# One block of step sizes cut into three steps and moved, and the q and k evictions raised in priority

## The chip, the cores and the metric

One core of a Trainium2 chip runs the whole kernel. The metric is the device time of one execution in microseconds (us). The core has five engines that each run their own instructions in an order fixed when the program is built: PE (TensorE, matrix products and transposes), ACT (ScalarE), DVE (VectorE), POOL (GpSimd) and SP (SyncE, which issues DMAs). Matrix products land in PSUM, eight banks in all; everything else lives in SBUF or in HBM.

## The reference, cut to what matters

One layer of a hybrid encoder is applied to two sequences, a prompt of 256 tokens and a sample of 512 tokens, with a model width of 1024. Three mixers (GLA, differential attention, SSD) read the same normalised input and their outputs go through one output product; an MLP with squared relu follows.

```
h = rmsnorm(x, norm1)
gq, gk, gv, gg, glr, dq, dk, dvv, sz, sxbc, sdt = split(h @ w_in)
o_gla  = gla_mixer(gq, gk, gv, gg, glr, ...)       # gated recurrence, both directions
o_diff = diff_mixer(dq, dk, dvv, ...)              # two softmaxes, w = p0 - lam * p1
o_ssd  = ssd_mixer(sz, sxbc, sdt, ...)             # state-space recurrence, both directions
x = x + concat(o_gla, o_diff, o_ssd) @ w_out
x = x + square(relu(rmsnorm(x, norm2) @ w_mlp1)) @ w_mlp2

# in ssd_mixer: the step sizes, and the running sums of their decay inside a chunk
dt = softplus(sdt + dt_bias)                       # 8 heads forward, 8 backward
la = dt * (-exp(a_log))
acum = cumsum(la)                                  # per chunk; exp(acum), exp(acum_last - acum) are used

# in gla_mixer: the gates
logg = log_sigmoid(r @ wg + bg) / 16               # forward and backward
```

## The kernel before, in words

The 768 tokens are six tiles of 128 (NT = 6): tiles 0 and 1 are the prompt, 2 to 5 the sample. Each fp32 product is made of three passes on values split in a high and a low part (`mm3`, L98 to L100). Weights come in halves (`wr`, L146) and are split by ACT (`wh`, L134) and DVE (`wl`, L135) in `load_unit`. The in-projection makes blocks of 256 columns, either transposed (`fm_unit`, features on partitions, two halves of 384 tokens) or by token (`tm_unit`, three blocks of two tiles). Their sums lie in the three PSUM banks called `acc`; all other PSUM results share five banks called `mx`.

The order of the stages in the program is: normalise and transpose x; `gla_v(0)`; `glr_unit`, which makes `rst` (the gates' low-rank input) and `zdt` (the raw step sizes, 16 rows at partitions 96 to 111); small vectors; `ssd_dt` (the block that the change is about); `gla_gates` for the two pairs of GLA heads; `gla_qk(0)`, the recurrence `gla_core` of pair 0, then q, k, v of pair 1, the output gate `gla_gate_out` of pair 0 (with a tanh), the recurrence of pair 1; for each of two pairs of attention heads the in-projection `diff_in(p)` and the two prompt heads; then the SSD (convolution, states, chunks), the output product, the sample heads, the MLP.

This program order is a priority, not the order on an engine. A planner puts every instruction on its engine's list as soon as, by its own costs, its operands and its tiles are there, and among those that could go it takes the one that stands first in the program; `tc.high_priority()` puts what is inside it ahead. `tc.issue_after` adds an order. Once built, each engine runs its list in order and waits on semaphores.

Tiles come from rings: `t3` (4 buffers of 776 columns), `s3` (6), `in` (12, made by the function `i3`, alive for the whole kernel), `s2` (3, opened when the GLA's rings are closed). A request waits until a buffer of its ring is free.

`ssd_dt` (L503 to L564) computes from `zdt`: Abs, Exp, Ln on ACT (L507 to L509); a correction of the logarithm on DVE with one more Exp (L510 to L514); the step sizes into `stk` (L517); times A into `dtl` (L520); a scan within each tile for the running sums `dpre` (L522), the exclusive sums `dexc` (L523); copies into `stk` (L524, L525) and differences (L527, `stb` L529). It then stores the sums to HBM: `scr` (L533, L534; read later by each SSD chunk as `ar` and `er`, L671 and L672) and the chunk totals `scp` (L535), reads `scp` back broadcast to all partitions as `ptb` (L538), takes its exponent on ACT (`decs`, L543), transposes `stk` and `stb` on PE into tokens by rows (L550, L555; three `mx` banks), copies them out on ACT (`tms` L552, `tmb` L556) and makes the factors `ew` (L558 to L563). `decs`, `tms` and `ew` are used by the SSD.

`gla_gates` (L268 on): matmuls `gate` (L274) into `mx` banks, Abs and Relu (L276, L277), Exp and Ln (L278, L279) on ACT, additions and a prefix scan on DVE (L282, L257). `gla_qk` evicts q and k from PSUM on ACT (L313). `gla_core`: transposes `kTp` (L371), then seven levels in each of which DVE makes `d` (L428) and `eq` (L433), POOL makes `ek` (L438), and PE many small matmuls `att` (L412). `diff_in` evicts each block to a tile `dqk` (L761) and squares it to `dsq` (L763), both from the ring `in`; DVE normalises and rotates (L765 to L775), and SP stores it; the `dv` blocks (L782) use the same ring. `diff_head` transposes q and k (`qT`, L811), makes scores `sc` (L835, L836), their row maximum (L837), exponent (`pr`, L838), the difference (L841), its transpose `wT` (L844), the product `O`, and in the end `ss` (L859) and `rb` (L867), all in `mx` banks.

Of the kernel before, what the change touches and what calls it, by code (L numbers as in the profile page):

```python
# [13 lines left out]
AF = mybir.ActivationFunctionType  # L14
ALU = mybir.AluOpType
# [4 lines left out]
P = 128  # L20
# [22 lines left out]
def hybrid_kernel(ctx, tc, io):  # L43
    nc = tc.nc
    mm, act, dve, pool = nc.tensor.matmul, nc.scalar, nc.vector, nc.gpsimd
# [14 lines left out]
    def tag(stack, name, bufs, width, side="left"):  # L60

        pl = stack.enter_context(tc.tile_pool(name=name, bufs=bufs, side=side, reuse_waits="tile"))

        def new(nme, dtype=F32, n=T if width == 776 else width):
            return pl.tile([P, width], dtype, tag=name, name=nm(nme))[:, :n]
        return new

    i3 = tag(ctx, "in", N_IN, 776)
# [4 lines left out]
    t3 = tag(first, "t3", N_T3, 776)  # L73
    c4 = tag(first, "c4", 6, 1024)
    s3 = tag(first, "s3", N_S3, 776)
# [17 lines left out]
    def bc(ap, shape):  # L93
        return ap.to_broadcast(shape)
# [99 lines left out]
    log_ins = []  # L194
# [29 lines left out]
        return [(raw[:, :, 0:32], w_in[:, :, C_GLR:C_GLR + 32]), (raw[:, :, 32:48], w_in[:, :, C_SDT:C_SDT + 16])]  # L224

    rst = s3("rst", F32R)
    zdt = s3("zdt")

    def glr_consume(ps, ts):
        act.copy(rst[0:96, ts], ps[0:96, :])  # L230
# [14 lines left out]
        fm_unit((gh, gl), 0, 112, glr_consume, halves_)  # L245


    resetm = s3("resetm")
    pool.memset(resetm, 1.0)
    pool.memset(resetm.rearrange("p (c w) -> p c w", w=P)[:, :, 0:1], 0.0)  # L250

    def v128(t):
        return t.rearrange("p (c w) -> p c w", w=P)

    def prefix(dst, lg):

        dve.tensor_tensor_scan(dst, resetm[:dst.shape[0]], lg, 0.0, ALU.mult, ALU.add)  # L257
# [49 lines left out]
    def gla_qk(hp):  # L307
        c0 = hp * P
        q, k = i3("gq"), i3("gk")

        def keep(dst, scale):
            def consume(ps, ts):
                act.activation(dst[:, ts], ps, AF.Copy, scale=scale)  # L313
            return consume

        w = load_unit(lambda r: [(0, P, w_in[:, r, C_GQ + c0:C_GQ + c0 + P]),
                                 (P, 2 * P, w_in[:, r, C_GK + c0:C_GK + c0 + P])], (KT, 256))
        fm_unit(w, 0, P, keep(q, 0.125), halves_)
        fm_unit(w, P, P, keep(k, 1.0), halves_)
        return q, k  # L320
# [181 lines left out]

    def ssd_dt():  # L503

        ps_ = slice(96, 112)
        z, t1, u, l = zdt[ps_], t3("dz")[ps_], t3("dt2")[ps_], t3("dl")[ps_]
        act.activation(t1, z, AF.Abs)  # L507
        act.activation(t1, t1, AF.Exp, scale=-1.0)
        act.activation(l, t1, AF.Ln, bias=1.0)  # L509
        dve.tensor_scalar(u, t1, 1.0, -1.0, op0=ALU.add, op1=ALU.add)  # L510
        dve.tensor_tensor(t1, t1, u, ALU.subtract)
        act.activation(u, l, AF.Exp, scale=-1.0)
        dve.tensor_tensor(t1, t1, u, ALU.mult)
        dve.tensor_tensor(l, l, t1, ALU.add)  # L514
        stk = t3("stk")
        pool.memset(stk, 0.0)
        dve.scalar_tensor_tensor(stk[0:16], z, 0.0, l, op0=ALU.max, op1=ALU.add)  # L517
        dtl = t3("dtl")[ps_]

        dve.tensor_scalar(dtl, stk[0:16], sdtc[0:16, 3:4], -128.0, op0=ALU.mult, op1=ALU.max)  # L520
        inc, exc = t3("dpre")[ps_], t3("dexc")[ps_]
        dve.tensor_tensor_scan(inc, resetm[ps_], dtl, 0.0, ALU.mult, ALU.add)  # L522
        dve.tensor_tensor(exc, inc, dtl, ALU.subtract)  # L523
        act.copy(stk[32:48], inc)  # L524
        act.copy(stk[64:80], exc)  # L525
        tot = bc(v128(inc)[:, :, 127:128], [16, NT, P])
        dve.tensor_tensor(v128(stk[96:112]), tot, v128(inc), ALU.subtract)  # L527
        stb = t3("stb")
        dve.tensor_tensor(v128(stb[0:16]), tot, v128(exc), ALU.subtract)  # L529

        scr = dram.tile([16, T], F32, name="scr")
        scp = dram.tile([16, NT], F32, name="scp")
        nc.sync.dma_start(out=scr[0:8, :], in_=inc[0:8])  # L533
        nc.sync.dma_start(out=scr[8:16, :], in_=exc[8:16])  # L534
        nc.sync.dma_start(out=scp, in_=v128(inc)[:, :, 127])  # L535

        ptb = const.tile([P, 2, 8, NT], F32, name="ptb")
        nc.sync.dma_start(out=ptb.rearrange("p d h c -> p (d h c)"),  # L538
                            in_=bc(scp.rearrange("h c -> (h c)")[None, :], [P, 16 * NT]))
        decs = const.tile([P, NT, 2, 4], F32, name="decs")  # L540
        for g in range(2):
            gs = slice(64 * g, 64 * g + 64)
            act.activation(decs[gs], ptb[gs, :, 4 * g:4 * g + 4, :].rearrange("p d h c -> p c d h"), AF.Exp)  # L543

        tms = const.tile([P, NT, 40], F32, name="tms")
        tmb = const.tile([P, NT, 16], F32, name="tmb")
        for (a, b) in ((0, 4), (4, 6)):
            ps = mx("tms")
            for c in range(a, b):
                nc.tensor.transpose(ps[:, (c - a) * P:(c - a) * P + 112], stk[0:112, c * P:(c + 1) * P], ident[0:112, 0:112])  # L550
            for o, r, n in ((0, 0, 16), (16, 32, 8), (24, 72, 8), (32, 96, 8)):
                act.copy(tms[:, a:b, o:o + n], v128(ps)[:, :b - a, r:r + n])  # L552
        ps = mx("tmb")
        for c in range(NT):
            nc.tensor.transpose(ps[:, 16 * c:16 * c + 16], stb[0:16, c * P:(c + 1) * P], ident[0:16, 0:16])  # L555
        act.copy(tmb, ps[:, :96].rearrange("p (c r) -> p c r", c=NT))  # L556
        ew = const.tile([P, NT, 2, 2, 8], F32, name="ew")
        act.activation(ew[:, :, 0, 0, :], tms[:, :, 16:24], AF.Exp)  # L558
        act.activation(ew[:, :, 0, 1, :], tmb[:, :, 8:16], AF.Exp)
        act.activation(ew[:, :, 1, 0, :], tms[:, :, 32:40], AF.Exp)  # L560
        act.activation(ew[:, :, 1, 1, :], tms[:, :, 24:32], AF.Exp)
        dve.tensor_tensor(ew[:, :, 1, 0, :], ew[:, :, 1, 0, :], tms[:, :, 0:8], ALU.mult)
        dve.tensor_tensor(ew[:, :, 1, 1, :], ew[:, :, 1, 1, :], tms[:, :, 8:16], ALU.mult)  # L563
        return scr, decs, tms, ew  # L564

    def ssd_conv(us, xt, bcm):
        def conv(j):
# [185 lines left out]
    def diff_in(p):  # L753

        for i, c0 in ((0, C_DQ), (1, C_DK)):
            w = in_unit(c0 + 256 * p)

            def cons(ps, t0):
                q = i3("dqk", n=512)
                with tc.high_priority():  # L760
                    act.copy(q.rearrange("p (t c) -> p t c", t=2), ps)  # L761
                sq = i3("dsq", n=512)
                act.activation(sq, q, AF.Square)  # L763
                ss, rs = small("dss", 8), small("drs", 8)
                dve.tensor_reduce(ss, hd(sq), AX.X, ALU.add)  # L765
                rstd_of(rs, ss, 8, 1.0 / 64)
                dve.tensor_tensor(hd(q), hd(q), bc(rs[:, :, None], [P, 8, 64]), ALU.mult)
                q4 = q.rearrange("p (t m d) -> p t m d", t=2, m=4)
                rab = sq[:, 0:256].rearrange("p (a t m d) -> p a t m d", a=2, t=2, m=4)
                ra, rb = rab[:, 0], rab[:, 1]  # L770
                ts = slice(t0, t0 + 2)
                dve.tensor_tensor(ra, q4[:, :, :, 0:16], bc(ropeg[:, i, 0, ts, None, :], [P, 2, 4, 16]), ALU.mult)
                dve.tensor_tensor(rb[:, :, :, 0:8], q4[:, :, :, 8:16], bc(ropeg[:, i, 1, ts, None, 0:8], [P, 2, 4, 8]), ALU.mult)
                dve.tensor_tensor(rb[:, :, :, 8:16], q4[:, :, :, 0:8], bc(ropeg[:, i, 1, ts, None, 8:16], [P, 2, 4, 8]), ALU.mult)
                dve.tensor_tensor(q4[:, :, :, 0:16], ra, rb, ALU.add)  # L775
                nc.sync.dma_start(out=(dqd, dkd)[i][p][t0 // 2], in_=q.rearrange("p (t c) -> p t c", t=2))
            tm_unit(w, cons)
        w = in_unit(C_DV + 256 * p)

        def vcons(ps, t0):  # L780
            v = i3("dv", n=512).rearrange("p (t c) -> p t c", t=2)
            act.copy(v, ps)  # L782
            nc.sync.dma_start(out=dvd[p][t0 // 2], in_=v)
        tm_unit(w, vcons)
# [87 lines left out]
    def take_turns(*steps):  # L872
        steps = list(steps)
        while steps:
            steps = [g for g in steps if next(g, g) is not g]
# [155 lines left out]
    qg8 = const.tile([P, 1], F32, name="qg8")  # L1031
    dve.tensor_scalar(qg8, col(R_QN), 0.125, None, op0=ALU.mult)

    dt = ssd_dt()
    pre = [gla_gates(hp) for hp in range(2)]

    masks = t2("masks").bitcast(U8)[:, :len(LOCAL) * 32].rearrange("p (l i) -> p l i", i=32)
# [30 lines left out]
    dve.tensor_scalar(nlam, nlam, -LAMBDA_INIT, None, op0=ALU.add)  # L1068

    qk = gla_qk(0)  # L1070
    core = gla_core(pre[0], qk, v)
    qk, v = gla_qk(1), gla_v(1)
    sg = gla_gate_out(0)
# [9 lines left out]
    dl = tag(second, "dl", N_DL, 512)  # L1083
    s2 = tag(second, "s2", N_S2, T)
# [7 lines left out]

    for p in range(2):
        diff_in(p)
        take_turns(*(diff_head(p, h, 0) for h in range(2)))
    xt, bcm = [None] * 4, [None] * 2
    tail = ssd_conv((2, 0, 1), xt, bcm)
# [126 lines left out]
```

## Time and profile before

| | |
|---|---|
| three runs of the kernel before | 1166.26, 1168.5, 1172.04 us (median 1168.5) |
| the profiled execution, its own time | 1169.03 us |
| its span, first to last instruction | 1167.2 us |
| mean granted TensorE clock | 0.976 |
| PE busy | 1110.8 us, 95% of the span |
| DVE, ACT, POOL busy | 63%, 48%, 13% |

The profile is one execution. All positions are us from the start of its span. The granted clock is 1.00 at 2.4 GHz; a stretch with part of its time at 1.2 GHz shows a value between 0.5 and 1. A row of a timeline gives start, duration, engine, line, operation, tiles and, in brackets, the idle time of the engine just before and what ended it. Matmuls overlap in the pipeline, so the distance of two starts, not the duration, is what one costs.

### The profile page before, as it was taken

How to read it: one execution, taken by the hardware profiler on the slowest of the kernel's cores; microseconds unless marked ns; L12 is line 12 of the kernel's file. 1: busy time of each engine (PE TensorE's matmuls, PEld its weight loads, DVE VectorE, ACT ScalarE, POOL GpSimd, SP SyncE). 2: the span in 40 equal slices, each digit the busy share in tenths (PEclk: the TensorE clock that was granted, in tenths of full speed). 3: DMA queues.
4: the chain of work that ended last, by engine and by line, in shares of the span. 5: the costliest groups of instructions: out<-in, count | busy, mean ns of one | idle time of the engine just before them, and what ended most of it. 6: DMA issues, size and time to landing. Idle time of an engine off the chain costs nothing.

```text
span 1167.2 us, 19741 instructions
## 1 busy us (share of the span) xinstructions
PE 1110.8 (95%) x7868; PEld 978.6 (84%) x7868; DVE 737.8 (63%) x1298; ACT 563.9 (48%) x1119; POOL 157.0 (13%) x208
## 2 busy tenths in 40 slices
PE   7989797999998999899989999999999999999998
PEld 6989697999998986788877897788887787787786
DVE  6559859563697668887677786846544534434443
ACT  7476666554377237756666573425231332322321
POOL 1002425310401360110100012200000000000000
PEclk9989798899999999899999999999999999999999
DMA  6312021171534355445543549522323323233231
GB/s 196 85 40 74 4 64 38 41 240 39 162 96 127 111 160 167 126 144 177 195 144 120 187 145 305 200 92 73 108 72 108 101 80 108 77 104 99 82 109 72
DMA packets 118642, 136.41 MB, mean 117 GB/s; under 512 B 8936, under 2 KB 86790, under 8 KB 118550
## 3 DMA queue, kind: packets, MB, share of 16 engines
q1 hardware_dynamic: 118517, 135.14, 36.6%
q8 instruction: 62, 1.02, 0.3%
q14 instruction: 31, 0.25, 0.1%
q10 hardware_dynamic: 32, 0.01, 0.0%
HBM read 121.44 MB, written 13.68 MB: 116 GB/s over the span
## 4 chain that ended last, share of the span: by engine, by line
PE 61%; DVE 16%; DMA 11%; ACT 6%; issue 3%; POOL 2%; SPq 0%; DVEq 0%; ACTq 0%; POOLq 0%
PE tp L98 7%; DMA wr<-in_w_mlp 7%; PE tp L99 7%; PE tp L100 7%; PE fm L98 6%; PE fm L100 6%; PE fm L99 6%; PE tm L100 5%; PE tm L99 5%; PE tm L98 5%; DVE wl L135 4%; ACT wh L134 2%; DMA er<-scr 1%; DVE d L428 1%; DVE eq L433 1%
## 5 line engine op out<-in xcount | busy, mean ns | idle before, releaser
L134 ACT CAST wh<-wr 128x1024 fp32r<-128x1024 f32 x186 | 189.2, 1048 | 236.5 <-PE tp L100 129.2
L135 DVE TENSOR_TENSOR wl<-wr,wh 128x1024 fp32r<-128x1024 f32 x186 | 224.2, 1229 | 93.4 <-ACT wh L134 92.8
L100 PE MATMUL tm<-wh,hTl 128*128 128x256 f32 x576 | 168.7, 293 | 0.0
L98 PE MATMUL tm<-wh,hTh 128*128 128x256 f32 x576 | 166.8, 290 | 0.5 <-ACT xp L576 0.5
L99 PE MATMUL tm<-wl,hTh 128*128 128x256 f32 x576 | 166.8, 290 | 0.0
L901 DVE TENSOR_TENSOR xres<-tp,xres 128x512 f32<-128x512 f32 x116 | 77.8, 687 | 100.5 <-PE tp L100 100.3
L99 PEld LDWEIGHTS tm<-wl,hTh 128*128 128x128 f32 x576 | 112.4, 195 | 1.5 <-issue 1.0
L98 PEld LDWEIGHTS tm<-wh,hTh 128*128 128x128 f32 x576 | 112.2, 195 | 1.6 <-ACT xp L576 0.8
L100 PEld LDWEIGHTS tm<-wh,hTl 128*128 128x128 f32 x576 | 112.4, 195 | 0.7 <-issue 0.4
L99 PE MATMUL fm<-h2l,wh 128*128 128x512 f32 (+1 forms) x288 | 107.5, 374 | 0.0
L98 PE MATMUL fm<-h2h,wh 128*128 128x512 f32 (+1 forms) x288 | 107.1, 373 | 0.3 <-ACT h2h L185 0.3
L100 PE MATMUL fm<-h2h,wl 128*128 128x512 f32 (+1 forms) x288 | 107.0, 372 | 0.0
L98 PE MATMUL tp<-wh,uh 128*128 128x512 f32 x256 | 101.7, 397 | 0.6
L99 PE MATMUL tp<-wl,uh 128*128 128x512 f32 x256 | 101.0, 395 | 0.0
L100 PE MATMUL tp<-wh,ul 128*128 128x512 f32 x256 | 99.7, 395 | 0.0
L98 PE MATMUL fm<-h,wh 128*128 128x256 f32 x256 | 72.5, 284 | 3.4 <-ACT relu L947 3.4
L99 PE MATMUL fm<-h,wh 128*128 128x256 f32 x256 | 72.7, 285 | 0.0
L100 PE MATMUL fm<-h,wl 128*128 128x256 f32 x256 | 72.0, 284 | 0.6 <-DVE wl L135 0.6
L947 ACT ACTIVATE relu<-fm 128x256 f32<-128x256 f32 (+1 forms) x68 | 31.7, 469 | 73.2 <-PE fm L100 73.2
L98 PEld LDWEIGHTS fm<-h2h,wh 128*128 128x128 f32 x288 | 54.7, 191 | 10.7 <-ACT h2h L185 0.5
L100 PEld LDWEIGHTS fm<-h2h,wl 128*128 128x128 f32 x288 | 55.0, 191 | 10.1
L99 PEld LDWEIGHTS fm<-h2l,wh 128*128 128x128 f32 x288 | 54.9, 191 | 10.1
(325 smaller groups left out, 2446.7 us busy)
## 6 DMA issues: line engine op xcount, KB each, us to landing
wr<-in_w_mlp SPq DMA_DIRECT2D x128, 512.0 KB
wr<-in_w_in SPq DMA_DIRECT2D x30, 512.0 KB
wr<-in_w_out SPq DMA_DIRECT2D x24, 512.0 KB
ar<-scr SPq DMA_DIRECT2D x6, 512.0 KB
er<-scr SPq DMA_DIRECT2D x6, 512.0 KB
x<-in_x_sample SPq DMA_DIRECT2D x4, 512.0 KB
wr<-in_w_in SPq DMA_DIRECT2D x8, 256.0 KB
xres<-in_x_sample SPq DMA_DIRECT2D x4, 512.0 KB
```

Of the source, the lines that this page charges most:

```text
L98: mm(out, lhsT=lh, rhs=rh, start=first, stop=False)
L99: mm(out, lhsT=lh, rhs=rl, start=False, stop=False)
L100: mm(out, lhsT=ll, rhs=rh, start=False, stop=last)
L134: act.copy(hi, raw)
L135: dve.tensor_tensor(lo, raw, rd(hi), ALU.subtract)
L428: dve.tensor_tensor(D[i].rearrange("p b r i -> p b (r i)"), X.rearrange("p (b i) -> p b i", i=2 * s), bc(ref, [P, nb, 2 * s]), ALU.subtract)
L433: dve.tensor_tensor(parts(eq)[:, :, i], D[i][:, :, i], parts(q)[:, :, i], ALU.mult)
L901: dve.tensor_tensor(xres[t][:, cs], ps, xres[t][:, cs], ALU.add)
L947: act.activation(r, ps, AF.Relu)
```

## The change

The tile of `zdt` comes from the ring `in`. The q and k evictions in `gla_qk` are put under high priority. `ssd_dt` becomes a generator of three steps. The first, Abs, Exp and Ln, is called after `gla_qk(0)`, and its Ln joins the list after which a tanh may be issued. The second, from the correction to the stores of `scr` and `scp`, is called after `diff_in(0)`; its tiles `dz`, `dl`, `dt2`, `stk`, `stb` come from the ring `in`, and `dpre`, `dexc` and a mask `reset` of its own (two POOL memsets) from the ring `s2`; `dtl` takes the tile of `dt2`. The third, from the load of `ptb` to `ew`, is called after `diff_in(1)`.

```diff
     rst = s3("rst", F32R)
-    zdt = s3("zdt")
+    zdt = i3("zdt")
...
-    resetm = s3("resetm")
-    pool.memset(resetm, 1.0)
-    pool.memset(resetm.rearrange("p (c w) -> p c w", w=P)[:, :, 0:1], 0.0)
...
+    def resets(t):
+        pool.memset(t, 1.0)
+        pool.memset(v128(t)[:, :, 0:1], 0.0)
+
+    resetm = s3("resetm")
+    resets(resetm)
...
         def keep(dst, scale):
             def consume(ps, ts):
-                act.activation(dst[:, ts], ps, AF.Copy, scale=scale)
+                with tc.high_priority():
+                    act.activation(dst[:, ts], ps, AF.Copy, scale=scale)
             return consume
...
         ps_ = slice(96, 112)
-        z, t1, u, l = zdt[ps_], t3("dz")[ps_], t3("dt2")[ps_], t3("dl")[ps_]
+        z, t1, l = zdt[ps_], i3("dz")[ps_], i3("dl")[ps_]
         act.activation(t1, z, AF.Abs)
         act.activation(t1, t1, AF.Exp, scale=-1.0)
-        act.activation(l, t1, AF.Ln, bias=1.0)
+        log_ins.append(act.activation(l, t1, AF.Ln, bias=1.0).ins)
+        yield
+        reset, u = s2("reset")[ps_], i3("dt2")[ps_]
+        resets(reset)
         dve.tensor_scalar(u, t1, 1.0, -1.0, op0=ALU.add, op1=ALU.add)
...
-        stk = t3("stk")
+        stk = i3("stk")
...
-        dtl = t3("dtl")[ps_]
+        dtl = u
...
-        inc, exc = t3("dpre")[ps_], t3("dexc")[ps_]
-        dve.tensor_tensor_scan(inc, resetm[ps_], dtl, 0.0, ALU.mult, ALU.add)
+        inc, exc = s2("dpre")[ps_], s2("dexc")[ps_]
+        dve.tensor_tensor_scan(inc, reset, dtl, 0.0, ALU.mult, ALU.add)
...
-        stb = t3("stb")
+        stb = i3("stb")
...
         nc.sync.dma_start(out=scp, in_=v128(inc)[:, :, 127])
+        yield
...
-        return scr, decs, tms, ew
+        yield scr, decs, tms, ew
...
-    dt = ssd_dt()
     pre = [gla_gates(hp) for hp in range(2)]
...
     qk = gla_qk(0)
+    dt_steps = ssd_dt()
+    next(dt_steps)
     core = gla_core(pre[0], qk, v)
...
     for p in range(2):
         diff_in(p)
+        dt = next(dt_steps)
         take_turns(*(diff_head(p, h, 0) for h in range(2)))
```

## Rows read from the trace of the kernel before

**Rows 1.** The page's busy times: us, share of the span, instructions of each engine.

```profile
PE 1110.8 (95%) x7868; PEld 978.6 (84%) x7868; DVE 737.8 (63%) x1298; ACT 563.9 (48%) x1119; POOL 157.0 (13%) x208
```

**Rows 2.** Stretches: length, busy PE, PEld, DVE, ACT, POOL, granted clock, DMA share, GB/s.

```profile
48.00:64.00 16.00, 16.00 (x97) 15.94 (x95) 12.66 (x23) 9.67 (x14) 1.51 (x4) 1.00 0.23 68
64.00:80.00 16.00, 12.27 (x60) 11.52 (x59) 2.33 (x5) 9.17 (x29) 0.00 (x0) 0.79 0.21 69
...
105.00:157.00 52.00, 44.53 (x965) 42.64 (x964) 37.77 (x60) 35.03 (x96) 19.14 (x13) 0.84 0.15 43
...
175.00:225.00 50.00, 41.22 (x962) 39.94 (x961) 34.75 (x51) 31.73 (x88) 18.00 (x16) 0.86 0.16 45
...
255.00:300.00 45.00, 45.00 (x387) 44.95 (x385) 20.19 (x45) 25.41 (x55) 0.69 (x1) 1.00 0.25 72
```

**Rows 3.** Two pieces of the chain of waits, 47 to 78: start, duration, what.

```profile
59.71 6.74 DMA scp<-dpre
...
66.51 4.25 DMA ptb<-scp
```

**Rows 4.** Timeline of PE, 62 to 78 us, first and last of each kind.

```profile
63.45 0.74 PE L550 MATMUL tms<-ident,stk 112*128 112x112 f32 x6
...
64.59 0.62 PE L274 MATMUL gate<-rst,wg 96*128 96x512 f32 x2
65.05 0.34 PE L98 MATMUL fm<-hTh,wh 128*128 128x384 f32 x1
...
67.84 0.34 PE L99 MATMUL fm<-hTl,wh 128*128 128x384 f32 x1
71.91 0.80 PE L274 MATMUL gate<-rst,wg 96*128 96x512 f32 x1 [3.73 <-ACT tms L552]
...
73.46 0.52 PE L98 MATMUL fm<-hTh,wh 128*128 128x384 f32 x1
73.78 0.52 PE L99 MATMUL fm<-hTl,wh 128*128 128x384 f32 x1
...
77.28 0.40 PE L274 MATMUL gate<-rst,wg 96*128 96x512 f32 x1
```

**Rows 5.** Timeline of ACT, 47 to 82 and 110 to 112 us.

```profile
63.11 0.48 ACT L313 ACTIVATE gk<-fm 128x384 f32<-128x384 f32 x1
70.78 0.58 ACT L543 ACTIVATE decs<-ptb 64x48 f32<-64x48 f32 x2 [7.20 <-DMA ptb<-scp]
...
110.67 1.28 ACT L198 ACT_TABLE_LOAD   x1
```

**Rows 6.** Timeline of DVE, 47 to 82 us.

```profile
47.47 0.55 DVE L231 TENSOR_TENSOR rst<-fm,rst 32x384 fp32r<-32x384 f32 x1
...
51.14 0.56 DVE L510 TENSOR_SCALAR dt<-dz 16x768 f32<-16x768 f32 x1 [0.52 <-ACT dz L508]
...
57.57 1.75 DVE L522 TENSOR_TENSOR_SCAN dpre<-resetm,dtl 16x768 f32<-16x768 f32 x1
...
61.21 0.95 DVE L529 TENSOR_TENSOR stb<-dpre,dexc 16x768 f32<-16x768 f32 x1
```

**Rows 7.** Timeline of PE, 446 to 448 us.

```profile
446.57 0.60 PE L727 MATMUL yT<-ident,y 128*128 128x128 f32 x4
447.00 1.26 PE L811 MATMUL qT<-ident,dqkv 128*128 128x128 f32 x10
```

**Rows 8.** Timelines of DVE and PE, 265 to 305 us, prompt heads.

```profile
265.86 0.48 DVE L841 SCALAR_TENSOR_TENSOR pr<-pr,dratio 128x256 f32<-128x256 f32 x1
...
268.71 0.38 PE L844 MATMUL wT<-ident,pr 128*128 128x128 f32 x2
...
303.91 0.59 PE L867 MATMUL rb<-dg,ones 128*128 128x256 f32 x2
```

**Rows 9.** Waits of PE, 45 to 330: us in total, times, longest us.

```profile
PE att L412 <- DVE eq L433: 9.3, 5, 3.0
```

**Rows 10.** Timeline of ACT, 306 to 307 us.

```profile
306.69 0.59 ACT L782 COPY dv<-tm 128x512 f32<-128x512 f32 x1 [6.01 <-DVE ms L158]
```

## Prediction

> **What bounds the kernel now.** I read the busy shares first: TensorE (PE) works 95% of the span [rows 1], so time can only come out of the places where PE stands still or runs slowly. The table of stretches shows where these are [rows 2]: from 48 to 64 us PE is full at the full clock; from 64 to 80 it is busy 12.27 of 16 us at a granted clock of 0.79; the two GLA recurrences (105 to 157 and 175 to 225) hold gaps and 0.84 and 0.86; from 255 to 300, under the differential attention's in-projection, PE is full at 1.00 again. The chain of waits of 47 to 78 us names what ends the hole at 64 to 80: two small DMAs, the last prefix column out to HBM (`scp`, 6.74 us) and its broadcast back (`ptb`, 4.25 us) [rows 3]. Then PE's own rows [rows 4]: the transposes of `stk` start at 63.45, two gate matmuls and 17 in-projection matmuls follow, and then PE idles 3.73 us until ACT has copied `tms` out. ACT could not copy because it stood 7.20 us at `decs` (L543), waiting for `ptb` [rows 5]. The gates need nothing of this: their input `rst` is complete at 47.47+0.55 = 48.0 [rows 6], yet their first matmul runs at 64.59, right behind the transposes. The gate banks come from the same five "mx" banks of PSUM, and `ssd_dt` asks first in program order. Elsewhere too a ready transpose of that ring waits for the one asked for earlier: qT follows yT by 0.43 us [rows 7].
>
> What the hole costs: 3.73 us idle, and what follows it at the low level. The 17 matmuls from 65.05 to 67.84 stand 2.79/16 = 0.174 us apart; at 73.46 and 73.78 they stand 0.32 apart, as after a fall from 2.4 to 1.2 GHz. The stretch from 71.91 to 77.28 holds 13 of them and four gate matmuls (two of 512 columns, two of 256). At the early rate that is 13 x 0.174 + (0.23+0.23+0.12+0.12) = 2.97 us, where 0.23 is half the time from 64.59 to 65.05. It took 5.37, so 2.40 are lost. **The hole costs 3.73 + 2.40 = 6.1 us** [rows 4].
>
> **The change part by part.** *The two holes' cause leaves the start.* `decs`, the eight `tms` copies and the ew work go behind the second in-projection call in program order, so ACT no longer waits there and the gates get their banks first: -6.1. The transposes (63.45 to 64.59, 1.14 us of PE) only move: 0.
>
> *The sums.* Ten DVE instructions of 0.56 to 1.75 us (L510 to L529; a scan is 1.75, most others 0.95 [rows 6]) leave the stretch 50 to 62, where PE was full: they gain nothing there by themselves. They arrive in the stretch from some 240 on, with three ACT instructions, a POOL memset of `stk`, two more POOL memsets (`reset`), and on SP the two `scr` stores and the `scp` store, queued among the `dqd`/`dkd` stores and the heads' fetches. DVE is busy 20.19 of 45 us there and ACT 25.41 [rows 2], so there is room; what is late next is a prompt head of the attention. Its weights `pr` are done by 265.86+0.48 = 266.34 and PE takes them at 268.71 [rows 8]: 2.37 us of slack in a step. What this costs is bounded below by 0 (PE is full at the full clock there, there is nothing to gain) and above by rival 2. I take one scan's length, 1.75 us, as exposed: the longest single instruction that can stand ahead of a head's reduction, and an end much nearer to 0, because slack and idle shares are both larger than one instruction.
>
> *The logarithms.* Abs, Exp and Ln stay early, three ACT instructions a few us later than now, behind evictions that PE does not wait for: 0. They stay ahead of the tanh of the gate, so no additional table load is in sight; the trace has one, at 110.67. If a second came, it would cost at most its own 1.28 us. [rows 5]
>
> *q and k evictions at high priority.* The last of them, at 63.11, came right behind two casts of 1 us [rows 5]; it may come 2.0 us earlier and the casts 0.5 later. PE had three banks to write into and never waited for it: between -0.5 and +0.5, taken as 0.
>
> *The rings.* `zdt`, `dz` and `dl` now hold three of the twelve "in" tiles from 50 us until the sums, and `stk` and `stb` two more until the transposes. Taken as 0; rival 3 prices it. `ar` and `er` of the SSD, which read `scr`, are fetched later, long before the SSD chunks: 0.
>
> **Sum.** 1169.03 (the profiled execution, span 1167.2) - 6.1 + 1.75 = 1164.7. That execution lies 0.5 above the median of 1168.5, so 1164.2 for a median. Its own range, with the return between 0 and 4.8 and 1 us of the kernel's own scatter: 1161 to 1168.
>
> **The rivals.** *One: the recurrences gain as well.* With 12 us of DVE work out of 50 to 62 and the gates computed from 48 on, the first recurrence can start as soon as q and k are there, up to 16 us (64.59 - 48.0) earlier. PE waits in the recurrences 9.3 us for DVE's `eq` [rows 9]. If half of this goes, with the same share of slow clock behind it as at the hole (2.40/3.73 = 0.64 us for each idle us), 4.65 x 1.64 = 7.6 us more: 1169.0 - 6.1 - 7.6 - 0.5 = 1154.8. For it: DVE and ACT idle at 64 to 80 (2.33 and 9.17 busy of 16). Against it: PE's order is fixed when the program is built, and the waits at `att` are steps of one serial chain between DVE, ACT and POOL, whenever it starts.
>
> *Two: the wait moves with the step.* `decs` stands in ACT's fixed order where the planner thinks `ptb` is there. It was off by 7.20 us here. If ACT stands as long among the prompt heads, a head's exponent and its eviction queue behind it: 7.20 - 2.37 of slack = 4.8 us of PE idle, and 4.8 x 0.64 = 3.1 of slow clock: 1169.0 - 6.1 + 7.9 - 0.5 = 1170.3. For it: ACT's rows now. Against it: the second half of the step is now asked for behind six evictions and the whole second in-projection, some 40 us of other work. It decides if `ptb` lands over 2.4 us later than ACT reaches `decs`.
>
> The two hops took 6.74 and 4.25 us here, 11.0 together [rows 3]. The Trainium skill ("DMA: Bandwidth & Descriptors", Anatomy of one DMA) gives some 2.0 us fixed for one transfer, nearly all of it the receipt of the target's write; by it the two hops would take about 4 us, the wait at `decs` would be 7 us shorter, near nothing, and rival two would give the forecast's own time. The rows say otherwise, and the rows price it.
>
> *Three, slower: the "in" ring runs short.* The second in-projection call takes twelve "in" tiles in six pairs, and its three `dv` evictions already wait for the first of them to come free: ACT idles 6.01 us before the one at 306.69 [rows 10]. With `stk` and `stb` held until the transposes, which come behind the heads' last use of the mx ring (303.91 [rows 8]), the sixth pair waits too. Its bank then comes free at about 304 + 1.1 of transposes + 0.6, when PE, three banks on, wants it at about 305: a stall of 0.7. Every us that the heads are later is added. If the sums' whole chain, 51.1 to 61.21+0.95, 11.0 us [rows 6], lies ahead of them, less 1 us of it beside the last stores, PE stalls 0.7 + 10.0 and loses 2.4 after it: 13.1. 1169.0 - 6.1 + 13.1 - 0.5 = 1175.5. Against it: the chain can run beside the end of the first in-projection call, from the moment the GLA pools are closed, ahead of the heads. It makes the kernel slower than before once the heads end over 3 us late (0.7 + 3 + 2.4 = 6.1).
>
> **How the numbers follow.** Forecast 0.38, rival one 0.24, rival two 0.22, rival three 0.16. About 0.5% (5.8 us) is what a measurement of this kernel can tell from no change: under 1162.7 counts as faster, over 1174.3 as slower. Faster: rival one and a third of the forecast, 0.24 + 0.13 = 0.37. Slower: 0.13 of rival three and a tail of rival two, 0.04, together 0.17. Within: 0.46. The range leaves out a tail of rival one (under 1153) and half of rival three (over 1175): 1153 to 1175; both signs hold weight, and the forecast's own range stands above.
>
> **What the profile after would show.** Right: first gate matmuls at about 50 us and no PE idle between 64 and 80; granted clock 1.00 there; `stk`'s transposes after 304; ACT's wait at `decs` under 2 us. Rival one: kTp well before 104 and less waiting at `att`. Rival two: ACT idle several us for `ptb` between 255 and 300, PE idle at wT. Rival three: ACT at L761 or L782 waiting for a tile and PE idle at 300 to 320 for a bank. The prediction is wrong if the gates still wait for something else of the early stage, a ring tile or q and k, so that the hole stays, or if the sums are planned earlier than the attention.

## The result and the profile after

The changed kernel takes 1176.39 us in the median of ten runs (1172.1 to 1179.0), the kernel before 1169.61 (1163.25 to 1172.17): the ratio is 1.0054, 95% interval 1.0034 to 1.0074, by which it is some 6.3 us longer. The forecast was 1164.2 with a range to 1175.0; the sign was wrong and the time lies just outside. The profiled execution is the fastest of the ten, 1172.1 us with a span of 1170.3, so its rows show less than the median's loss.

Read the stretches first. The table of the changed kernel, its columns those of [rows 2]:

```profile
48.00:64.00 16.00, 16.00 (x94) 15.82 (x93) 7.78 (x18) 13.12 (x24) 0.94 (x4) 1.00 0.22 68
64.00:80.00 16.00, 16.00 (x97) 16.00 (x96) 13.60 (x16) 14.44 (x27) 3.88 (x12) 1.00 0.21 66
80.00:105.00 25.00, 24.29 (x368) 23.69 (x369) 19.58 (x25) 13.04 (x32) 8.29 (x7) 1.00 0.14 44
105.00:157.00 52.00, 45.90 (x871) 45.16 (x859) 38.97 (x66) 34.56 (x89) 14.25 (x19) 0.93 0.20 58
175.00:225.00 50.00, 43.50 (x937) 42.39 (x936) 35.75 (x76) 28.44 (x75) 23.11 (x20) 0.90 0.16 53
255.00:300.00 45.00, 37.70 (x301) 37.45 (x301) 17.76 (x37) 17.46 (x39) 0.70 (x1) 0.89 0.30 73
300.00:325.00 25.00, 23.36 (x165) 22.81 (x164) 19.75 (x61) 13.11 (x37) 13.78 (x19) 1.00 0.45 148
325.00:400.00 75.00, 66.61 (x435) 65.73 (x434) 54.88 (x100) 43.03 (x98) 4.67 (x14) 0.95 0.37 109
```

Three stretches of the kernel before that did not stand among its rows:

```profile
80.00:105.00 25.00, 25.00 (x202) 25.00 (x200) 24.65 (x27) 19.96 (x37) 3.92 (x13) 1.00 0.15 43
300.00:325.00 25.00, 25.00 (x178) 24.84 (x179) 18.76 (x54) 9.71 (x18) 12.16 (x22) 1.00 0.59 193
325.00:400.00 75.00, 71.64 (x479) 69.18 (x478) 57.93 (x105) 44.78 (x99) 9.31 (x17) 0.98 0.34 107
```

Against [rows 2]: the hole at 64 to 80 is gone (16.00 busy at 1.00, where 12.27 at 0.79 stood), and PE idles 12.6 instead of 16.3 us in the two stretches of the recurrences, but 0.7 us at 80 to 105, where the first recurrence now begins. Then it comes back: 7.3 us of idle time at 255 to 300, where the kernel before had none, 1.6 at 300 to 325, and 8.4 instead of 3.4 at 325 to 400. In sum, 3.7 and 3.7 gained, 0.7, 7.3, 1.6 and 5.0 lost.

The early start is in PE's timelines: the first gate matmul and the first `kTp` of the changed kernel, then the first `kTp` of the kernel before.

```profile
51.55 1.09 PE L277 MATMUL gate<-rst,wg 96*128 96x512 f32 x5
...
89.41 0.82 PE L375 MATMUL kTp<-ident,kst 128*128 128x128 f32 x6
```

```profile
104.36 0.82 PE L371 MATMUL kTp<-ident,kst 128*128 128x128 f32 x6
```

The 7.3 us are one wait. ACT's timeline, then DVE's and PE's, then pieces of the chain of waits, all of the changed kernel:

```profile
261.13 0.63 ACT L772 ACTIVATE dsq<-dqk 128x512 f32<-128x512 f32 x1
270.32 0.58 ACT L552 ACTIVATE decs<-ptb 64x48 f32<-64x48 f32 x2 [8.57 <-DMA ptb<-scp]
270.93 0.37 ACT L857 CAST wt<-wT 128x256 fp32r<-128x256 f32 x1
...
273.71 0.47 ACT L847 ACTIVATE pr<-sc,dmx 128x256 f32<-128x256 f32 x1
```

```profile
272.89 2.36 DVE L135 TENSOR_TENSOR wl<-wr,wh 128x1024 fp32r<-128x1024 f32 x2 [1.13 <-ACT wh L134]
...
275.61 0.48 DVE L850 SCALAR_TENSOR_TENSOR pr<-pr,dratio 128x256 f32<-128x256 f32 x1
```

```profile
276.15 0.69 PE L853 MATMUL wT<-ident,pr 128*128 128x128 f32 x2 [7.30 <-DVE pr L850]
```

```profile
257.61 6.49 DMA scp<-dpre
264.17 6.14 DMA ptb<-scp
...
277.70 0.21 PE tm L100
...
281.61 0.12 PE tm L98
```

It is the wait of [rows 5] again, in another place: ACT comes to `decs` at 261.8 and stands 8.57 us, since the store of `scp` (6.49) and the read back (6.14) take 12.6. Behind it in ACT's list stand a head's eviction, a block's eviction, two casts `wh` and the exponents `pr`. DVE's list holds the wait up further: two `wl`, which need those casts, stand ahead of the last step of `pr` (L850), and PE waits for that. From 276.15 to 281.3 most of PE's matmuls stand 0.21 us apart instead of 0.12, at the lower clock (0.50 from 276.2 to 281.2).

The losses after 300 are spread. PE's waits from 300 to 400 us, of the changed kernel (engine and line, for whom, us, times, longest):

```profile
PE xtmp L607 <- DVE zh L603: 5.2, 1, 5.2
PE tm L98 <- ACT xp L585: 3.2, 1, 3.2
PE rb L876 <- DVE ms L158: 1.2, 1, 1.2
PE tm L98 <- ACT dqk L770: 0.4, 1, 0.4
```

Three of them are places where DVE or ACT is late in the convolution or with the second in-projection's evictions; `rb` belongs to the end of a head. What is new there is in ACT's timeline:

```profile
305.87 0.48 ACT L561 COPY tms<-tms 128x64 f32<-128x64 f32 x4 [2.23 <-PE tms L559]
306.21 0.63 ACT L770 COPY dqk<-tm 128x512 f32<-128x512 f32 x1
...
307.09 2.52 ACT L683 ACTIVATE er<-er,tms 128x128 f32<-128x128 f32 x8
309.44 0.69 ACT L772 ACTIVATE dsq<-dqk 128x512 f32<-128x512 f32 x1
```

Copies of `tms` and the `er` work of the first sample chunk stand between the sixth `dqk` eviction and its square. In the kernel before that work ran at 242:

```profile
242.30 2.45 ACT L674 ACTIVATE er<-er,tms 128x128 f32<-128x128 f32 x8 [1.44 <-DMA er<-scr]
```

### The profile page after: what moved, and what is told of

Read it like the earlier page. It is cut to its first block, busy times and chain, and to the rows that moved or that the text cites. A ratio compares the mean times of both kernels' runs of the same rounds, so it can differ in the third digit from the quotient of the medians.

```text
span 1170.3 us, 19757 instructions
## 1 busy us (share of the span) xinstructions
PE 1108.7 (95%) x7868; PEld 979.4 (84%) x7868; DVE 740.7 (63%) x1298; ACT 564.2 (48%) x1119; POOL 158.0 (13%) x210
## 4 chain that ended last, share of the span: by engine, by line
PE 74%; DVE 9%; DMA 7%; ACT 5%; issue 3%; POOL 2%; SPq 0%; DVEq 0%; ACTq 0%; POOLq 0%
PE fm L98 9%; PE fm L99 9%; PE fm L100 9%; PE tp L98 8%; PE tp L99 8%; PE tp L100 8%; PE tm L98 4%; PE tm L100 4%; PE tm L99 4%; DMA wr<-in_w_mlp 3%; DVE wl L135 2%; DMA er<-scr 2%; ACT wh L134 1%; DVE eq L437 1%; POOL wx L658 1%
## 5 line engine op out<-in xcount | busy, mean ns | idle before, releaser
L98 PE MATMUL tm<-wh,hTh 128*128 128x256 f32 x576 | 169.4, 294 | 3.7 <-ACT xp L585 3.2
L98 PEld LDWEIGHTS tm<-wh,hTh 128*128 128x128 f32 x576 | 114.9, 200 | 5.1 <-ACT xp L585 3.5
L99 PEld LDWEIGHTS tm<-wl,hTh 128*128 128x128 f32 x576 | 114.8, 199 | 0.6 <-DVE wl L135 0.2
L100 PEld LDWEIGHTS tm<-wh,hTl 128*128 128x128 f32 x576 | 115.0, 200 | 0.3
```

The lines of the kernel that those rows point to most:

```text
L98: mm(out, lhsT=lh, rhs=rh, start=first, stop=False)
L99: mm(out, lhsT=lh, rhs=rl, start=False, stop=False)
L100: mm(out, lhsT=ll, rhs=rh, start=False, stop=last)
```

## Experiments

Ratios are to the kernel before on the same chip, with 95% intervals. The runs were made on several chips, so a difference of two runs in us is the difference of their ratios, times 1170.

**The wait at decs, in both kernels.** Two runs move only the two exponents of `decs` on ACT. In the first the order of everything else stays; in the second a handful of neighbours move too.

before_decs_late:

```diff
-            act.activation(decs[gs], ptb[gs, ...], AF.Exp)
...
-        return scr, decs, tms, ew
+        return (scr, decs, tms, ew), ptb
...
-    dt = ssd_dt()
+    dt, ptb = ssd_dt()
     pre = [gla_gates(hp) for hp in range(2)]
+    with tc.issue_after(log_ins[-1]):
+        for g in range(2):
+            act.activation(dt[1][gs], ptb[gs, ...], AF.Exp)
```

> The kernel before, with only the two exponents of decs moved on ACT behind the logarithm of the last gate; every other engine's order is unchanged. If the hole at 68 to 72 us is ACT standing at decs for the second DMA, the eight tms copies run at about 64.5, PE's idle 3.73 us there goes to 0 and the slow stretch behind it (2.4 us) with it: 1169.6 - 6.1 = 1163.5 us. If the gates' chain on ACT and DVE is what PE would wait for next, PE idles again before 80 us and the time stays within 1167 to 1170.

Measured: 1164.69 us, ratio 0.9946 (0.9925 to 0.9967), 6.3 us less, where 6.1 were worked out. Its stretches:

```profile
64.00:80.00 16.00, 16.00 (x99) 15.64 (x98) 8.19 (x12) 14.67 (x39) 0.11 (x1) 1.00 0.20 70
105.00:157.00 52.00, 44.47 (x976) 42.48 (x974) 38.54 (x70) 33.86 (x94) 19.26 (x12) 0.87 0.09 26
175.00:225.00 50.00, 41.33 (x948) 39.89 (x947) 34.93 (x64) 28.98 (x80) 21.26 (x18) 0.83 0.09 24
```

The hole is closed, the transposes still stand at 64 us and the recurrences idle as before (16.2 us). So the hole's cause is `decs` alone, not the sums or the transposes, and the prediction's price of it fits this run. Another run below closes the same hole for less.

after_decs_late:

```diff
-            act.activation(decs[gs], ptb[gs, ...], AF.Exp)
...
+        last_ew = act.activation(ew[:, :, 1, 1, :], tms[:, :, 24:32], AF.Exp)
+        with tc.issue_after(last_ew.ins):
+                act.activation(decs[gs], ptb[gs, ...], AF.Exp)
```

> The changed kernel, with only the two exponents of decs put behind the last exponent of ew on ACT. Theory A, the wait for the two DMAs moved with the step: ACT's idle 8.57 us at decs goes, PE's idle 7.3 us at wT (276 us) goes, and 2 to 2.5 us of slow clock behind it: 1176.4 - 9.5 = 1167. Theory B, the sums on DVE and the held tiles delay the prompt heads and what follows: PE idles at another head or for a bank between 255 and 310, and the time stays over 1173.

Measured: 1170.12 us, ratio 0.9992 (0.9976 to 1.0008), 7.3 us less than the changed kernel. Stretches:

```profile
255.00:300.00 45.00, 43.76 (x372) 43.51 (x371) 24.06 (x50) 19.62 (x43) 1.58 (x3) 1.00 0.28 76
...
325.00:400.00 75.00, 66.50 (x424) 65.35 (x423) 52.54 (x97) 43.28 (x96) 4.49 (x11) 0.91 0.34 99
```

Theory A is right for the first loss: at 255 to 300 the idle time falls from 7.3 to 1.2 and the clock is 1.00. But 8.5 us of idle time stay at 325 to 400. The whole change without this wait is no faster than the kernel before, and 5.4 us slower in the median than before_decs_late, which moves two instructions.

**The priority of the q and k evictions.** after_qk_plain:

```diff
-                with tc.high_priority():
-                    act.activation(dst[:, ts], ps, AF.Copy, scale=scale)
+                act.activation(dst[:, ts], ps, AF.Copy, scale=scale)
```

> The changed kernel without the high priority of the q and k evictions. Built, its engines have the same instructions in the same order as with it. Both theories expect the time of the changed kernel, 1176.4, so this run shows what two programs of one order differ by (under 3 us).

Measured: 1179.63 us, ratio 1.0078 (1.0050 to 1.0105). The instructions and their order are the same with and without it on all five engines; this part of the change does nothing. The distance to 1.0054 is what two builds of one order differ by here; the two intervals meet.

**What else is late after 300 us.** decs_late_er_late, on top of after_decs_late:

```diff
+                    xt_copies.append(act.copy(xt[j][:, a:b, :], ...).ins)
...
+            with tc.issue_after(xt_copies[1]) if c == 2 else ExitStack():
                 act.activation(er[:, h], er[:, h], AF.Identity, ...)
```

> As after_decs_late, and the er and ar work of the first sample chunk (8 ACT and 8 DVE instructions and one exponent, which ran at 302 to 308 us there, in the middle of the second in-projection's rotation, and at 236 to 246 in the kernel before) held back on ACT until the first xt copies are done. Theory B1, this work on ACT and DVE delays the rotation, the second pair of heads and the convolution: the last rotation step ends 4 to 5 us sooner (315 instead of 320), PE's idle 5.2 at xtmp and 3.2 at xp shrink by over half, and the time falls by 4 to 6 us against after_decs_late, to 0.995 of the kernel before. Theory B2, the ring of twelve tiles (stk and stb hold two) delays the sixth pair: the last rotation stays near 320 and the time within 2 us of after_decs_late.

Measured: 1164.02 us, ratio 0.9940 (0.9918 to 0.9961), about 6 us less than after_decs_late, with intervals that do not meet. The hold moves more than the 16 instructions: from 302 us on the planner puts PE's, ACT's and DVE's work in another order too, so the run tests the hold with all that it brings. The profiled execution, 1168.93 us, is the slowest of its seven. DVE's last rotation step, in after_decs_late and then in this run:

```profile
320.39 0.28 DVE L785 TENSOR_TENSOR dqk<-dsq 128x128 f32<-128x128 f32 x1
```

```profile
313.11 0.48 DVE L788 TENSOR_TENSOR dqk<-dsq 128x128 f32<-128x128 f32 x2
```

The rotation ends 7 us sooner, and PE's waits for the convolution (xtmp and xp), 5.2 and 3.2 us in after_decs_late as in the changed kernel, shrink to 4.4:

```profile
PE xtmp L610 <- DVE zh L606: 4.4, 2, 2.9
PE wT L857 <- DVE pr L854: 1.8, 1, 1.8
```

decs_late_stk_sc:

```diff
-        stk = i3("stk")
+        stk = sc("stk", n=T)
...
-        stb = i3("stb")
+        stb = sc("stb", n=T)
```

> As after_decs_late, with stk and stb in the ring sc (two tiles, used otherwise by the sample chunks' ar and er) instead of the ring in; the sample chunk's ar and er are then loaded after the transposes. Theory B2: the sixth dqk eviction comes at about 288 to 293 instead of 301 and the time falls by 4 to 6 us against after_decs_late, to 0.995 of the kernel before. Theory B1 expects a gain too, but only as large as that of decs_late_er_late, since the er and ar work moves here as well: what this run gains over that one is the ring's.

Measured: 1169.54 us, ratio 0.9984 (0.9969 to 0.9999). The sixth eviction does come at 282.08 instead of 301.14, so the two tiles were what it waited for; the time does not follow. In its place PE waits 4.5 us for `dv` evictions, and ACT stands 2.56 us ahead of two of them, at `er`, whose load this edit puts behind the transposes:

```profile
282.08 0.59 ACT L771 COPY dqk<-tm 128x512 f32<-128x512 f32 x1 [2.75 <-PE tm L100]
...
309.26 2.45 ACT L684 ACTIVATE er<-er,tms 128x128 f32<-128x128 f32 x8 [2.56 <-DMA er<-scr]
```

```profile
PE fm L98 <- ACT dv L792: 4.5, 2, 2.3
PE xtmp L608 <- DVE zh L604: 4.4, 2, 2.9
```

The ring's shortage is real. What it costs by itself this run does not show, since the edit brings a wait of its own. decs_er_late_sc has both edits:

> decs_late_stk_sc (0.9984) with the sample chunk's er and ar work also held behind the first xt copies. If that work beside the rotation is what costs (theory B1), this gains 3 to 6 us: 0.994. If the ring counts as well, it goes below decs_late_er_late, to about 0.991, and the sixth dqk eviction stays at 282. If neither, it stays at 0.998.

Measured: 1167.14 us, ratio 0.9959 (0.9944 to 0.9974). With the hold on `er` the time is some 3 us less again, but the intervals meet. The two tiles add nothing that shows, since decs_late_er_late without them is at 0.9940. The ring is still short one step later: ACT waits for the store of a `dqk` tile before it can evict `dv`.

```profile
311.39 1.07 ACT L795 COPY dv<-tm 128x512 f32<-128x512 f32 x2 [3.68 <-DMA dqd<-dqk]
```

decs_late_er_last holds `er` until the last `xt` copy (`xt_copies[7]`):

> As decs_late_er_late, with the sample chunk's er and ar work held behind the last xt copy (about 390 us) instead of the first pair (about 350). If this work is what still delays the convolution there (PE idle 4.4 at xtmp and 1.8 at wT, against 1.8 in before_decs_late), those fall by 2 to 4 us and the time goes from 0.994 to about 0.991 of the kernel before. If the sums' and the transposes' new place costs them in another way (later heads), the time stays within 0.002 of 0.994.

Measured: 1168.87 us, ratio 0.9974 (0.9956 to 0.9993): no further gain; its interval meets that of decs_late_er_late, and also that of after_decs_late. PE's wait at xtmp falls from 4.4 to 2.9 us, and one of 2.6 at `rb` comes in. after_er_late is the hold on `er` in the changed kernel, with `decs` left in its place:

> The changed kernel with the er and ar work of the first sample chunk held back alone, decs left where the change puts it. If the two causes are separate, this gains what er late gained beside decs late, 0.005 of the time (6 us): from 1.0054 to about 1.000 of the kernel before, and PE's 7.3 us at wT for decs stays. If the er work only mattered because something else was late, it gains less than 2 us.

Measured: 1175.96 us, ratio 1.0036 (1.0020 to 1.0052), some 2 us less than the changed kernel, with intervals that meet; PE's wait at `wT` for `decs` stays, 8.3 us. The 6 us that two separate causes would give are not seen; why is not shown. before_decs_er_late is the hold in before_decs_late:

> before_decs_late (0.9946) with the sample chunk's er and ar work held behind the first xt copies, so that it runs at about 345 to 350 us, where the moved sums put it in decs_late_er_late, instead of 236 to 246. If having this work late costs by itself, the time rises by 2 to 4 us, to 0.997; if it is hidden there, it stays within 0.0015 of 0.9946, and what the changed kernel lost was its place beside the rotation.

Measured: 1168.33 us, ratio 0.9972 (0.9958 to 0.9986). It points to a cost of 3 us for having this work late at all, and PE idles 5.5 us at 325 to 400 where before_decs_late has 3.3, 2.6 of it at `ss`; but the interval meets that of before_decs_late (to 0.9967), so it is not settled.

**Whether an earlier start of the gates is worth anything.** before_gates_first, on top of before_decs_late:

```diff
-    dt, ptb = ssd_dt()
     pre = [gla_gates(hp) for hp in range(2)]
+    dt, ptb = ssd_dt()
```

> The kernel before_decs_late, with the gates ahead of the whole block of step sizes in program order; nothing is moved to a later stage. If the gates' wait for the mx banks is what holds the recurrences back, the gate matmuls run at about 50 instead of 64.6 us, the first kTp comes up to 10 us earlier than its 98 us, and the time falls by 2 to 5 us against before_decs_late (0.9946 of the kernel before). If the recurrences' waits do not depend on when they start, the time stays within 1.5 us of it.

Measured: 1173.07 us, ratio 1.0016 (1.0002 to 1.0031), 8 us slower than before_decs_late. The gates did run at 50.36, but the first kTp came at 103.38 instead of 98.18:

```profile
50.36 1.09 PE L274 MATMUL gate<-rst,wg 96*128 96x512 f32 x5
```

```profile
103.38 0.90 PE L371 MATMUL kTp<-ident,kst 128*128 128x128 f32 x3 [5.04 <-DVE kst L363]
```

DVE's timeline says why: the sums now run from 75 to 88 us, and then the recurrence's `eb` waits for a tile of the ring t3 that the store of `dexc` still reads.

```profile
87.34 0.95 DVE L529 TENSOR_TENSOR stb<-dpre,dexc 16x768 f32<-16x768 f32 x1
93.64 0.96 DVE L348 TENSOR_TENSOR eb<-tot,pre 128x768 f32<-128x768 f32 x1 [5.35 <-DMA scr<-dexc]
```

So the early start of the changed kernel (gates at 51.55, kTp at 89.41) is not had by the order of gates and sums alone; there the sums are out of the way as well.

**How long the two transfers have to be.** One edit, made in each of the two kernels; DVE first collects the chunk totals in 16 rows of 6 neighbouring values:

```diff
-        nc.sync.dma_start(out=scp, in_=v128(inc)[:, :, 127])
+        ends = const.tile([P, NT], F32, name="ends")
+        dve.tensor_copy(ends[ps_], v128(inc)[:, :, 127])
+        nc.sync.dma_start(out=scp, in_=ends[ps_])
```

> The changed kernel, with the chunk totals first copied by DVE to 16 rows of 6 neighbouring values, so that the store scp moves 16 pieces of 24 bytes instead of 96 of 4 bytes. If the number of pieces makes it slow, scp takes 2 to 3 us instead of 6.5, ACT's wait at decs falls from 8.6 to about 5, and the time falls by about 4 us against the changed kernel (1.0054 of the kernel before). If a store and its reading back take this long whatever their pieces, scp stays over 5.5 us and the time does not change.

Measured: 1170.51 us, ratio 0.9991 (0.9972 to 1.0011), 7 us less than the changed kernel. Pieces of its chain, then ACT at `decs`:

```profile
261.38 4.20 DMA scp<-ends
265.64 3.69 DMA ptb<-scp
```

```profile
269.35 0.30 ACT L554 ACTIVATE decs<-ptb 64x48 f32<-64x48 f32 x1 [2.06 <-DMA ptb<-scp]
```

The two take 7.9 instead of 12.6 us; ACT's wait at `decs` is 2.1 us. That is not what the shorter transfer did, though. The store starts at 261.38 instead of 257.61, so `ptb` is there only 1.0 us sooner (269.35 instead of 270.32). The rest of the 6.5 us is ACT's order: with the added instruction the planner puts two evictions, the two casts `wh`, a square and a `pr` ahead of `decs`, and ACT comes to it at 267.3 instead of 261.8. So this run gains mostly as after_decs_late does, by `decs` standing later, and does not price the transfer.

> The kernel before, with the chunk totals copied by DVE to 16 rows of 6 neighbouring values ahead of the store scp; nothing else moves on any engine. By the changed kernel's run of this edit scp takes 4.2 instead of 6.5 us (2.3 to 2.5 less) and the read back 3.7 to 4.3, and the added DVE copy about 0.2: ACT's wait at decs falls from 7.2 to about 5, PE's idle 3.73 to about 1.5, and the time falls by 2 to 4 us (0.997 of the kernel before). If the transfer's length was chance there, scp stays at 6 to 7 us and the time does not move.

Measured: 1167.75 us, ratio 0.9970 (0.9954 to 0.9985), as expected. Here the order of PE, ACT, DVE and POOL stays but for the added copy; on SP the store now stands behind the second store of `scr` instead of ahead of it. SP, ACT and the stretch of the hole:

```profile
62.15 0.31 SPq L537 DMA_DIRECT2D scp<-ends  x1
63.48 0.35 SPq L540 DMA_DIRECT2D ptb<-scp  x1
```

```profile
67.36 0.60 ACT L545 ACTIVATE decs<-ptb 64x48 f32<-64x48 f32 x2 [2.92 <-DMA ptb<-scp]
```

```profile
64.00:80.00 16.00, 16.00 (x98) 15.64 (x97) 6.59 (x10) 13.00 (x37) 0.11 (x1) 1.00 0.22 70
```

The read back is issued 1.33 us after the store, where it was 6.8 in [rows 3] (66.51 less 59.71); ACT waits 2.92 instead of 7.20, and PE is busy all of 64 to 80 at the full clock. The hole is closed as in before_decs_late, for 3.5 us instead of 6.3; the two intervals meet (0.9954 to 0.9967).

## Why the prediction was wrong, point by point

**The hole's cause was right, and its price about right.** 3.73 + 2.40 = 6.1 by [rows 4]; before_decs_late gives 6.3 for the removal of the wait alone, before_one_row, which closes the same hole, 3.5. Both intervals allow 3.9 to 5.4 us.

**The gain of the recurrences, rival one, was partly right.** kTp comes 15 us sooner. PE idles 3.7 us less in the two stretches, 2.9 with the stretch from 80 to 105, where 4.65 were supposed; over the other runs with the same early order it is 0.4 (after_er_late) to 3.2 (decs_late_er_last). The slow clock behind it, priced at 3.0, is not settled: the changed kernel shows 0.93 and 0.90, after_decs_late with the same early order 0.80 and 0.86.

**The step that failed first is the return of 1.75 us.** It took the place of rival two's wait because "the second half of the step is now asked for behind six evictions and the whole second in-projection". That reads program order as time. The planner puts an instruction in the first gap of its engine at which, by its own costs, the operands are there; ACT had gaps among the heads, and ACT came to `decs` at 261.8, over 40 us ahead of the transposes that stand beside it in the program. The prediction's own text had the contrary in hand: "It was off by 7.20 us here". Rival two's mechanism is what happened, at 0.22. Its price was 4.8 idle and 3.1 slow; measured 7.3, and, from 24 matmuls at the lower clock, some 2.4. The term that was mis-sized is the slack: 2.37 us were taken off 7.20, but only 1.3 of the 8.57 were absorbed, since two evictions and two casts had piled up on ACT behind `decs` by then, and on DVE the two `wl` that need these casts. And the transfers took 12.6 instead of 11.0 us; SP had issued the load of `ar`, 512 KB, between the two, at 258.90, and whether that made them longer was not tested. The rule of the Trainium skill weighed there ("DMA: Bandwidth & Descriptors", Anatomy of one DMA), some 2.0 us for a transfer, is fitted there to transfers that GpSimd issues, and these two were issued by SP. By it this wait would have vanished; the measurement decides against it for these two as they stand (6.49 and 6.14 us), and the stores of whole rows (1.33 and 4.20 us) come to both sides of it.

**The second, likely, is the zero for `ar` and `er`.** They were "fetched later, long before the SSD chunks: 0". True of the fetch; but 8 ACT instructions (2.52 us) and 8 on DVE hang on `tms`, had run at 242 to 245, and now fall right behind the transposes, in the rotation that the second pair of heads waits for. Held back, 6 us come back in one pair of runs. In the three others it is 2 to 3, with intervals that meet, about what two builds of one order differ by, and the hold reorders other work as well. So the place of the loss is shown (8.4 us of PE's idle time at 325 to 400 instead of 3.4), and the share of this work in it is not.

**Rival three named a real shortage and the wrong price.** The sixth pair did wait for `stk` and `stb` (306.21 instead of 293.31 us), and removing that in decs_late_stk_sc, where other waits took its place, moved no time that shows. Its figure of 1175.5 is near the median by chance.

**The logarithms and the high priority** were rightly taken as 0: PE is full from 48 to 80 us, and the latter is the same program.

**Open.** With `decs` late and `er` held back, PE still idles 6.3 us at 325 to 400 where before_decs_late has 3.3. before_decs_er_late, where the sums have not moved, has 5.5, so much of this may be the late `er` work itself; the moved transposes, copies and sums were not told apart from it. No version with the sums moved is shown to be faster than before_decs_late, where everything stays but two instructions.

## What to carry to other kernels

Where a list scheduler places work by its own costs, moving a block to a later stage need not take its waits away: an instruction that waits for a DMA goes wherever the planner believes the data to be there, and blocks its engine wherever that belief is wrong. First ask which single instruction holds the queue, and order that one behind work that is late anyway; here moving two instructions gave what the whole move was after. A small edit can make the planner reorder others; compare the orders before a gain is put down to the edit, as after_one_row shows. When a block is moved, list also what reads its results elsewhere: that work moves with it.

## What the runs showed of the hardware

The store of 96 separate 4-byte values took 6.74 and 6.49 us; as 16 rows of 24 bytes it took 4.20 in one kernel and at most 1.33 in the other, with the same 384 bytes. The store's place among SP's issues differs as well: where it took 4.20, the load of `ar` was issued 0.56 us ahead of it. So the pieces are not shown to be the whole of the difference. The copy that makes the rows is one small DVE instruction (0.16 us). Two builds with one and the same order on all engines gave ratios of 1.0054 and 1.0078, so a difference of a quarter per cent or less is not told from none here.
